# Moving two operand tiles by 128 bytes within a partition of SBUF

## The chip, the cores and the metric

The kernel runs on one core of one Trainium2 chip. The metric is the time of one execution on the device, in microseconds (us).

## The reference

A block of a streaming encoder on 512 tokens of 1024 channels, in float32, with the batch and the depth at 1. Two branches work on the same normed tokens and are merged by gates:

```python
h = rms_norm(x, norm_gain)
proj = einsum('bsd,dc->bsc', h, w_in)            # 1024 -> 10240 columns
sb_q, sb_k, sb_v, sb_g, r_q, r_k, r_v, r_g, m_sb, m_ret = split(proj)

# stick-breaking attention, 8 heads of 128
z = einsum(q, k) * 128 ** -0.5                   # q, k normed per head
log_keep = where(s < t, log_sigmoid(-z), 0)
w = where(s < t, exp(log_sigmoid(z) + sum_later(log_keep)), 0)
out_a = (w @ v) * silu(sb_g)

# retention, 4 heads of 256, rotary q and k, decay gamma_h ** |t - s|,
# causal by chunks of 64
out_b = rms_norm(retention(q, k, v)) * silu(r_g)

p_a, p_b = out_a @ w_branch_sb, out_b @ w_branch_ret
merged = sigmoid(m_sb + b0) * p_a + sigmoid(m_ret + b1) * p_b
out = x + merged @ w_out
```

## The kernel before, in words

Every large product is made in float32r from operands split into two parts, hi and lo: `mm3` (L89) issues three matmuls, hi x hi, hi x lo and lo x hi, into one bank of PSUM. All matmuls go through `matmul` (L84) and all transposes through `transpose` (L87), both kept in the order of the program, so the order of TensorE's work is that of the code.

The transposed tokens are loaded once (`first_loads`, L143), scaled by the gain and split into the two constant tiles xT_hi and xT_lo, each 128 partitions by 8 x 512 values, 16 KB in a partition (L140, L141). They stay for the whole kernel.

`dense` (L209) makes a group of 512 columns: four banks of PSUM, for each of the eight blocks k of 128 channels four times three matmuls, 96 in all, each with 128 x 128 stationary and 128 x 512 moving values. The weights of a group come from `load_split` (L189): pairs of 128 rows are loaded by SyncE's queue into raw, cast to hi by ScalarE and subtracted to lo by VectorE (`split`, L111 to L114), each in two buffers. With rows=True the activations are stationary and the weights moving, otherwise the other way round:

- groups that multiply the tokens (`proj`, L237): qk (4 groups), v and rv (2 each), with the tokens stationary; sg, ma, rg and mb (2 each) and rqk (4), with the tokens moving;
- groups that don't: pa and pb, with the branches' results oa and ob moving; fin, with the merged tokens mg stationary.

Between the pairs of steps of `dense`, `work.step()` takes pieces of side work from a list (`Interleaver`, L38): the transposes of q and k (pqk), the scores of attention (z), the transposes of its weights (pw) and its products with v (po), the scores of retention (rz), its products (ro) and the transposes of its results (rt). Which piece comes where is fixed by counts in the code, not by time. Transposes have a data tile as stationary operand and the constant tile ident as moving one.

Where a tile lies in its partition follows from the order of the `.tile` calls of the constant pool (bufs=1), and behind it the pools wpool (weights), big, tmp and small. Each tile begins at the next multiple of 32 bytes. The order of the constant tiles is wT_0, wT_1 (8192 bytes each), zero, warm (4 bytes each), vec (V_N = 34 values, 136 bytes), xT_hi, xT_lo (16384 each), idle (1024), ident (512), neg_mask (512), m_half (16 values, 64 bytes), rx, rx2 (16 each), rb, cr, sr (2048 each). All tiles of wpool and big are 2048, 4096 or 8192 bytes, so they all begin at the same residue modulo 512.

Of the kernel before, what the change touches and what calls it, by code (L numbers as in the profile page):

```python
# [7 lines left out]
F32 = mybir.dt.float32  # L8
# [4 lines left out]
P = 128  # L13
# [13 lines left out]

V_NG, V_BM, V_QG, V_KG, V_RG, V_N = 0, 8, 24, 25, 26, 34


RAW_BUFS = 2
V_BUFS = 14
# [3 lines left out]


class Interleaver:  # L38
    """Emits a dense stream of products step by step, with pieces of side work between the steps."""

    def __init__(self):
        self.side = []
# [23 lines left out]
def hybrid_block(ctx, tc, x, x_t, vecs, w_in, w_a, w_b, w_o, cos_t, sin_t, decay, out):  # L66
    nc = tc.nc
    PSUM = bass.MemoryType.PSUM

    const = ctx.enter_context(tc.tile_pool(name="const", bufs=1))  # L70
# [7 lines left out]
    work = Interleaver()  # L78
# [8 lines left out]
        tc.keep_in_program_order(nc.tensor.transpose(*a))  # L87

    def mm3(ps, a, b, first, last):  # L89
        """ps += a.T @ b for a and b in two parts each."""  # L90
        matmul(ps, a[0], b[0], start=first, stop=False)
        matmul(ps, a[0], b[1], start=False, stop=False)
        matmul(ps, a[1], b[0], start=False, stop=last)
# [23 lines left out]
        tc.keep_in_program_order(nc.sync.dma_start(dst, src))  # L117

    def load_weights(dst, w, k, n, blocks):
        """n times 128 rows of w, one block of columns or two equal ones."""  # L120
        rows = w[k * P : (k + n) * P, :].rearrange("(a p) c -> p a c", p=P)
        c0, width = blocks[0]
        if len(blocks) == 1:
            load(dst, rows[:, :, c0 : c0 + width])
            return
        step = blocks[1][0] - c0
        for a in range(n):
            src = rows[:, a, c0 - c0 % step : c0 - c0 % step + 2 * step].rearrange("p (b c) -> p b c", b=2)
            load(
                dst[:, a, :].rearrange("p (b c) -> p b c", b=2),  # L130
                src[:, :, c0 % step : c0 % step + width],
            )
# [3 lines left out]
    warm = const.tile([P, 1], F32, name="warm")  # L136
    nc.scalar.activation(warm, zero, AF.Sigmoid)

    vec = const.tile([P, V_N], F32, name="vec")
    xT_hi = const.tile([P, NK, S], F32R, name="xT_hi")  # L140
    xT_lo = const.tile([P, NK, S], F32R, name="xT_lo")  # L141

    def first_loads():  # L143
        """The transposed tokens, and the first weights between them."""
        raws = [wpool.tile([P, 2, S], F32, tag="raw", bufs=RAW_BUFS, name=f"first_raw{k}") for k in range(2)]
        xt = [T_tile(f"xt{hf}", F32) for hf in range(2)]
        for k in range(NK):
            ks = slice(k * P, (k + 1) * P)
            if k < 4:
                load_weights(raws[k // 2][:, k % 2 : k % 2 + 1, :], w_in, k, 1, ((C_Q, 256), (C_K, 256)))  # L150
            load(xt[k // 4][:, k % 4, :], x_t[ks, :])
            if k == 0:
                load(vec, vecs)
        for k in range(NK):
            r = xt[k // 4][:, k % 4, :]
            g = vec[:, V_NG + k : V_NG + k + 1]
            nc.scalar.activation(xT_hi[:, k, :], r, AF.Copy, scale=g)  # L157
            nc.vector.scalar_tensor_tensor(
                xT_lo[:, k, :], r, g, f32(xT_hi[:, k, :]), op0=ALU.mult, op1=ALU.subtract
            )  # L160
        return raws

    first = first_loads()
# [14 lines left out]
    )  # L178
    for t in wT_pair:
        nc.vector.tensor_copy(t[:, NT - 1, (NT - 2) * P : (NT - 1) * P], zero.broadcast_to([P, P]))  # L180
    m_half = const.tile([P, 16], F32, name="m_half")
    nc.gpsimd.memset(m_half, -0.5)

    def rsqrt(dst, ssq, n, width):
# [2 lines left out]
        nc.gpsimd.tensor_tensor(dst, t[:, :width], m_half[:, :width], op=ALU.pow)  # L187

    def load_split(name, w, blocks):  # L189
        """The weights of a group by pairs of 128 rows, in two parts."""  # L190
        for k in range(0, NK, 2):
            with tc.high_priority():
                if name == "qk0" and k < 4:
                    raw = first[k // 2]
                else:
                    raw = wpool.tile([P, 2, S], F32, tag="raw", bufs=RAW_BUFS, name=f"{name}_raw{k}")
                    load_weights(raw, w, k, 2, blocks)
                hi = wpool.tile([P, 2, S], F32R, tag="whi", name=f"{name}_hi{k}")
                lo = wpool.tile([P, 2, S], F32R, tag="wlo", name=f"{name}_lo{k}")
                if name == "qk0" and k < 4:  # L200
                    for j in range(2):
                        nc.vector.tensor_copy(hi[:, j, :], raw[:, j, :])
                        nc.vector.tensor_sub(lo[:, j, :], raw[:, j, :], f32(hi[:, j, :]))
                else:
                    split(hi, lo, raw)
            for j in range(2):
                yield k + j, hi[:, j, :], lo[:, j, :]

    def dense(name, act, w, blocks, rows):  # L209
        """Four PSUM banks: act.T @ w by row blocks, or by column blocks transposed."""  # L210

        ps = [ps_mm.tile([P, S], F32, tag="mm", name=f"{name}_ps{j}") for j in range(4)]
        late = []
        for k, hi, lo in load_split(name, w, blocks):
            if name == "fin1" and k >= NK - 2:
                late.append((k, act(k), (hi, lo)))
                continue
            ahi, alo = act(k)
            if name == "qk0" and k < 2:
                for a, b in ((ahi, hi), (ahi, lo), (alo, hi)):  # L220
                    for j in range(4):
                        matmul(ps[j], a[:, j * P : (j + 1) * P], b, start=k == 0 and a is ahi and b is hi, stop=False)
                continue
            for j in range(4):
                js = slice(j * P, (j + 1) * P)
                if rows:
                    mm3(ps[j], (ahi[:, js], alo[:, js]), (hi, lo), k == 0, k == NK - 1)
                else:
                    mm3(ps[j], (hi[:, js], lo[:, js]), (ahi, alo), k == 0, k == NK - 1)
                if j % 2 == 1 and not (k == NK - 1 and j == 3):  # L230
                    work.step()
        for j in range(4 if late else 0):
            for k, a, b in late:
                mm3(ps[j], [t[:, j * P : (j + 1) * P] for t in a], b, False, k == NK - 1)
        return ps
# [28 lines left out]
        yield 1  # L264

    def token_norm_rows():
        """The tokens' factors along the columns, the same in all partitions."""
        load(cr, cos_t)
        load(sr, sin_t)
        yield 5  # L270
        pr = side_psum("pr")
        for tb in range(NT):
            rc = tmp.tile([P, P], F32, tag="rc", bufs=2, name="rc")
            nc.vector.tensor_copy(rc, rx[:, tb : tb + 1].broadcast_to([P, P]))
            matmul(pr[:, tb * P : (tb + 1) * P], rc, ident, start=True, stop=True)
        nc.vector.tensor_copy(rb, pr)
        nc.gpsimd.tensor_mul(cr, cr, rb)
        nc.gpsimd.tensor_mul(sr, sr, rb)
        yield 1
# [1 line left out]
    qk_parts = {}  # L281

    def qk_group(p):
        """Heads 2p, 2p+1: normed, transposed q and k in two parts: [d, (q0 q1 k0 k1), t]."""
        ps = proj(f"qk{p}", ((C_Q + 256 * p, 256), (C_K + 256 * p, 256)), True)
        ss = small.tile([P, NT, 4], F32, tag="ss", name=f"ss{p}")
        raws = []
# [38 lines left out]
            work.add(token_norm_rows())  # L326

    def v_group(name, c0):
        """Rows of v in two parts, each [s, 512 columns] by row block."""
        ps = proj(name, ((c0, S),), True)  # L330
        got = []
        for sb in range(NT):
            hi = big.tile([P, S], F32R, tag="V", bufs=V_BUFS, name=f"{name}_hi{sb}")
            lo = big.tile([P, S], F32R, tag="V", bufs=V_BUFS, name=f"{name}_lo{sb}")
            r = rx[:, sb : sb + 1]
            nc.scalar.activation(hi, ps[sb], AF.Copy, scale=r)
            nc.vector.scalar_tensor_tensor(lo, ps[sb], r, f32(hi), op0=ALU.mult, op1=ALU.subtract)
            got.append((hi, lo))
        return got
# [25 lines left out]
    oa = {}  # L365

    def attention(heads, ready, v, gates):
        """Stick-breaking attention of some heads, their blocks of 128 queries in a pipeline."""
        blocks = [(h, b) for h in heads for b in range(NT)]
        beta = {}  # L370

# [53 lines left out]
                yield W_W  # L425

    def rope_group(h):
        """Rotated q and k of a head, transposed, in two parts: [d, (q q' k k'), t]."""
        banks = proj(f"rqk{h}", ((C_RQ + 256 * h, 256), (C_RK + 256 * h, 256)), False)
        ps = banks[:2]  # L430
        hi, lo = T_tile(f"rqk_hi{h}"), T_tile(f"rqk_lo{h}")
# [87 lines left out]
    v, sg, rv, rg = {}, {}, {}, {}  # L519
# [17 lines left out]
    for g in range(2):  # L537
        m = gate_group(f"ma{g}", C_MA + S * g, V_BM + 4 * g)
        ps = dense(f"pa{g}", branch_act(oa), w_a, ((S * g, S),), False)
        t = T_tile(f"pa{g}", F32)  # L540
# [26 lines left out]
    for g in range(2):  # L567
        m = mb[g]
        ps = dense(f"pb{g}", branch_act(ob), w_b, ((S * g, S),), False)
        hi, lo = T_tile(f"mg_hi{g}"), T_tile(f"mg_lo{g}")  # L570
        for j in range(4):
            t = tmp_tile(f"mg{g}_{j}")
# [6 lines left out]
    for g in range(2):  # L579
        ps = dense(f"fin{g}", lambda k: tuple(t[:, k % 4, :] for t in mt[k // 4]), w_o, ((S * g, S),), True)  # L580
# [67 lines left out]
```

## Time and profile before

| | |
|---|---|
| median of 3 runs | 671.56 us (670.75 to 671.97) |
| the profiled execution's own time | 671.6 us |
| its span | 671.6 us |
| TensorE busy | 664.3 us, 99% |
| VectorE / ScalarE / GpSimd busy | 375.5 / 260.9 / 50.0 us |
| HBM read | 62.41 MB |

The busy time of TensorE counts a matmul from its start to its modelled end, and matmuls overlap: a matmul of 512 columns is given as some 390 ns, while the next one begins after a little more than half of that. How fast a stretch goes is read from the starts, or from the length of an unbroken stretch divided by the number of its matmuls. A timeline row with "x3" merges three instructions in a row, its time reaching from the first start to the last end.

### The profile page before, as it was taken

Reading aid. Unit: us, or ns where it says so; the run is one execution under the profiler, and the core shown is the slowest. Engines: PE = TensorE matmul, PEld = TensorE weight load, DVE = VectorE, ACT = ScalarE, POOL = GpSimd, SP = SyncE. Lnnn points to the kernel's source line nnn. Section 1 sums busy time; section 2 is a strip of 40 time slices with the busy share of each in tenths; the row PEclk is TensorE's granted clock in tenths of the full one; section 3 lists DMA queues with packets and bytes.
Section 4 is the critical chain, followed back from the end, with each engine's and each line's share of the span. In section 5 each row is a group of like instructions: output and inputs, shape, how many; then the busy total and the mean of one; then the engine's idle time right before and its main releaser. Section 6 shows DMA issues by size and latency. Waiting matters only on the chain.

```text
span 671.6 us, 7979 instructions
## 1 busy us (share of the span) xinstructions
PE 664.3 (99%) x3096; PEld 546.3 (81%) x3096; DVE 375.5 (56%) x560; ACT 260.9 (39%) x416; POOL 50.0 (7%) x50
## 2 busy tenths in 40 slices
PE   8999999999999999999999999999999999999997
PEld 5888888888888888888888888888888888888886
DVE  6346773587487477632333763843863853444632
ACT  4743544464354464421322342433432433422310
POOL 0041000431000300000000001001001001000000
PEclk9999999999999999999999999999999999999999
DMA  8532213222312323132233323222313222234441
GB/s 276 194 125 78 81 62 95 89 69 64 95 62 63 94 63 95 58 99 95 94 95 110 95 63 93 83 91 80 95 63 99 82 86 63 95 94 158 156 157 62
DMA packets 42182, 65.02 MB, mean 97 GB/s; under 512 B 2848, under 2 KB 19488, under 8 KB 42144
## 3 DMA queue, kind: packets, MB, share of 16 engines
q1 hardware_dynamic: 41568, 63.47, 30.3%
q10 hardware_dynamic: 576, 1.05, 0.4%
q8 instruction: 24, 0.39, 0.2%
q14 instruction: 14, 0.11, 0.1%
HBM read 62.41 MB, written 2.10 MB: 96 GB/s over the span
## 4 chain that ended last, share of the span: by engine, by line
PE 98%; DMA 1%; SPq 0%; ACT 0%; DVE 0%; issue 0%; DVEq 0%; ACTq 0%
PE qk_ps L84 14%; PE rqk_ps L84 13%; PE rg_ps L84 7%; PE ma_ps L84 7%; PE mb_ps L84 7%; PE sg_ps L84 7%; PE rv_ps L84 7%; PE v_ps L84 7%; PE pa_ps L84 6%; PE pb_ps L84 6%; PE fin_ps L84 6%; PE po L84 2%; PE rz L84 2%; PE z L84 2%; PE ro L84 2%; PE pw L87 1%
## 5 line engine op out<-in xcount | busy, mean ns | idle before, releaser
L84 PE MATMUL qk_ps<-qk_hi,xT_hi 128*128 128x512 f32 x128 | 51.8, 413 | 2.0 <-ACT xT_hi L157 2.0
L84 PE MATMUL rqk_ps<-xT_hi,rqk_hi 128*128 128x512 f32 x128 | 51.0, 398 | 0.0
L84 PE MATMUL rqk_ps<-xT_hi,rqk_lo 128*128 128x512 f32 x128 | 50.5, 395 | 0.0
L84 PE MATMUL rqk_ps<-xT_lo,rqk_hi 128*128 128x512 f32 x128 | 50.5, 395 | 0.0
L84 PE MATMUL qk_ps<-qk_lo,xT_hi 128*128 128x512 f32 x128 | 50.3, 402 | 0.0
L84 PE MATMUL qk_ps<-qk_hi,xT_lo 128*128 128x512 f32 x128 | 49.6, 395 | 0.0
L84 PE MATMUL pa_ps<-oa,pa_hi 128*128 128x512 f32 x128 | 39.4, 389 | 0.0
L84 PE MATMUL pb_ps<-ob,pb_hi 128*128 128x512 f32 x128 | 39.4, 389 | 0.0
L114 DVE TENSOR_TENSOR rqk_lo<-rqk_raw,rqk_hi 128x1024 fp32r<-128x1024 f32 x16 | 20.6, 1288 | 24.4 <-ACT rqk_hi L113 24.4
L384 DVE TENSOR_TENSOR_SCAN keep<-keep,zero 128x128 f32<-128x128 f32 (+3 forms) x32 | 27.1, 846 | 7.3 <-ACT keep L382 7.3
L84 PEld LDWEIGHTS qk_ps<-qk_hi,xT_hi 128*128 128x128 f32 x128 | 24.5, 192 | 7.7 <-ACT xT_hi L157 2.9
L84 PEld LDWEIGHTS qk_ps<-qk_hi,xT_lo 128*128 128x128 f32 x128 | 24.3, 190 | 5.7
L84 PEld LDWEIGHTS rqk_ps<-xT_hi,rqk_lo 128*128 128x128 f32 x128 | 24.1, 188 | 5.7
L84 PEld LDWEIGHTS qk_ps<-qk_lo,xT_hi 128*128 128x128 f32 x128 | 24.7, 193 | 4.7
L84 PEld LDWEIGHTS rqk_ps<-xT_lo,rqk_hi 128*128 128x128 f32 x128 | 24.1, 188 | 5.2
L84 PEld LDWEIGHTS rqk_ps<-xT_hi,rqk_hi 128*128 128x128 f32 x128 | 24.1, 188 | 5.2
L84 PEld LDWEIGHTS pa_ps<-oa,pa_hi 128*128 128x128 f32 x128 | 24.0, 188 | 5.1
L84 PEld LDWEIGHTS pb_ps<-ob,pb_hi 128*128 128x128 f32 x128 | 24.0, 188 | 5.0
L187 POOL TENSOR_TENSOR rrr<-ms,m_half 128x4 f32<-128x4 f32 x4 | 4.0, 1006 | 321.5 <-DVE ms L186 321.5
L113 ACT CAST rqk_hi<-rqk_raw 128x1024 fp32r<-128x1024 f32 x16 | 16.8, 1047 | 26.4 <-PE rqk_ps L84 17.0
L114 DVE TENSOR_TENSOR qk_lo<-qk_raw,qk_hi 128x1024 fp32r<-128x1024 f32 x14 | 17.3, 1235 | 16.3 <-ACT qk_hi L113 16.3
L84 PE MATMUL v_ps<-v_hi,xT_hi 128*128 128x512 f32 x64 | 26.3, 411 | 0.0
(185 smaller groups left out, 1711.9 us busy)
## 6 DMA issues: line engine op xcount, KB each, us to landing
rqk_raw<-in_w_in SPq DMA_DIRECT2D x32, 256.0 KB, 3.0
qk_raw<-in_w_in SPq DMA_DIRECT2D x28, 256.0 KB, 3.1
v_raw<-in_w_in SPq DMA_DIRECT2D x8, 512.0 KB, 3.7
sg_raw<-in_w_in SPq DMA_DIRECT2D x8, 512.0 KB, 3.7
rv_raw<-in_w_in SPq DMA_DIRECT2D x8, 512.0 KB, 3.7
ma_raw<-in_w_in SPq DMA_DIRECT2D x8, 512.0 KB, 3.7
pa_raw<-in_w_a SPq DMA_DIRECT2D x8, 512.0 KB, 3.7
rg_raw<-in_w_in SPq DMA_DIRECT2D x8, 512.0 KB, 3.7
```

The source lines that it names most:

```text
L84: tc.keep_in_program_order(nc.tensor.matmul(*a, **k))
L87: tc.keep_in_program_order(nc.tensor.transpose(*a))
L113: nc.scalar.copy(hi, src)
L114: nc.vector.tensor_sub(lo, src, f32(hi))
L187: nc.gpsimd.tensor_tensor(dst, t[:, :width], m_half[:, :width], op=ALU.pow)
L384: nc.vector.tensor_tensor_scan(keep[:, :n][:, ::-1], keep[:, :n][:, ::-1], zero.broadcast_to([P, n]), 1.0, op0=ALU.mult, op1=ALU.add,)
```

## The change

The constant tiles vec and m_half are allocated wider, and their first columns are used as before. vec takes 66 values (264 bytes) in place of 34, m_half 112 values (448 bytes) in place of 16. With steps of 32 bytes xT_hi, xT_lo, idle, ident, neg_mask and m_half begin 128 bytes later, and all tiles behind m_half 512 bytes later. Some comments (docstrings) are taken out as well, each leaving an empty line.

```diff
 V_NG, V_BM, V_QG, V_KG, V_RG, V_N = 0, 8, 24, 25, 26, 34
 
+V_ROOM, M_ROOM = 66, 112
+
...
-    vec = const.tile([P, V_N], F32, name="vec")
+    vec = const.tile([P, V_ROOM], F32, name="vec")[:, :V_N]
     xT_hi = const.tile([P, NK, S], F32R, name="xT_hi")
     xT_lo = const.tile([P, NK, S], F32R, name="xT_lo")
...
-    m_half = const.tile([P, 16], F32, name="m_half")
+    m_half = const.tile([P, M_ROOM], F32, name="m_half")[:, :16]
     nc.gpsimd.memset(m_half, -0.5)
```

## Rows read from the trace of the kernel before

**Rows 1.** The page: span, busy time by engine, the chain's shares.
```profile
span 671.6 us, 7979 instructions
...
PE 664.3 (99%) x3096; PEld 546.3 (81%) x3096; DVE 375.5 (56%) x560; ACT 260.9 (39%) x416; POOL 50.0 (7%) x50
...
PE 98%; DMA 1%; SPq 0%; ACT 0%; DVE 0%; issue 0%; DVEq 0%; ACTq 0%
```

**Rows 2.** TensorE's waits: total us, times, longest.
```profile
PE qk_ps L84 <- ACT xT_hi L157: 2.0, 1, 2.0
PE pi L84 <- DVE idle L166: 1.2, 1, 1.2
```

**Rows 3.** The chain's longest pieces: start us, us, what, matmuls.
```profile
98.48 25.10 PE qk_ps L84 x108
167.40 12.60 PE sg_ps L84 x54
...
301.98 22.39 PE ma_ps L84 x96
324.37 21.77 PE pa_ps L84 x96
346.14 22.39 PE rqk_ps L84 x96
...
624.08 43.53 PE fin_ps L84 x192
```

**Rows 4.** Windows: busy PE, PEld, DVE, ACT, POOL, clock, DMA share, GB/s.
```profile
301.80:324.20 22.40, 22.40 (x97) 18.02 (x96) 7.68 (x9) 5.35 (x6) 0.00 (x0) 1.00 0.30 95
324.20:346.00 21.80, 21.80 (x98) 18.04 (x97) 7.65 (x9) 5.64 (x8) 0.00 (x0) 1.00 0.31 96
```

**Rows 5.** Groups by line and form: xcount, busy us, mean ns.
```profile
L84 PE MATMUL qk_ps<-qk_hi,xT_hi 128*128 128x512 f32 x128 | 51.8, 413 | 2.0 <-ACT xT_hi L157 2.0
...
L87 PE MATMUL pw<-ident,beta 128*128 128x128 f32 x80 | 13.9, 272 | 0.0
...
L84 PEld LDWEIGHTS rqk_ps<-xT_hi,rqk_hi 128*128 128x128 f32 x128 | 24.1, 188 | 5.2
L84 PEld LDWEIGHTS pa_ps<-oa,pa_hi 128*128 128x128 f32 x128 | 24.0, 188 | 5.1
...
L87 PEld LDWEIGHTS pw<-ident,beta 128*128 128x128 f32 x80 | 10.5, 140 | 3.6
```

**Rows 6.** Timeline of PE, the start: start us, us, instruction.
```profile
6.79 2.08 PE L84 MATMUL qk_ps<-qk_hi,xT_hi 128*128 128x512 f32 x4 [2.01 <-ACT xT_hi L157]
...
10.37 1.21 PE L84 MATMUL qk_ps<-qk_hi,xT_lo 128*128 128x512 f32 x4
```

**Rows 7.** Timeline of PE: first and fifth triple of pa0, each from its start.
```profile
280.01 0.62 PE L84 MATMUL pa_ps<-oa,pa_hi 128*128 128x512 f32 x2
...
282.77 0.62 PE L84 MATMUL pa_ps<-oa,pa_hi 128*128 128x512 f32 x2
```

**Rows 8.** Timeline of PE: six score matmuls of retention, then rg.
```profile
380.97 0.39 PE L84 MATMUL rz<-rqk_hi 128*128 128x512 f32 x1
...
381.67 0.39 PE L84 MATMUL rz<-rqk_hi 128*128 128x512 f32 x1
...
382.35 0.40 PE L84 MATMUL rg_ps<-xT_hi,rg_hi 128*128 128x512 f32 x1
```

**Rows 9.** Timeline of PE: first and last cut into xT groups.
```profile
43.48 0.60 PE L87 MATMUL pqk<-ident,qraw 128*128 128x128 f32 x4
...
575.75 0.60 PE L87 MATMUL rt<-ident,roraw 128*128 128x128 f32 x4
```

**Rows 10.** Timelines of ACT and DVE: one pair of weights in ma1.
```profile
307.37 1.05 ACT L113 CAST ma_hi<-ma_raw 128x1024 fp32r<-128x1024 f32 x1 [4.54 <-PE ma_ps L84]
...
308.46 1.23 DVE L114 TENSOR_TENSOR ma_lo<-ma_raw,ma_hi 128x1024 fp32r<-128x1024 f32 x1 [4.37 <-ACT ma_hi L113]
```

**Rows 11.** Timeline of DVE at the start: third pair of qk0.
```profile
16.16 1.22 DVE L114 TENSOR_TENSOR qk_lo<-qk_raw,qk_hi 128x1024 fp32r<-128x1024 f32 x1 [0.88 <-ACT qk_hi L113]
```

## The prediction

> **What bounds the kernel now.** I read the page first: TensorE is busy for 664.3 of 671.6 us, and it makes up 98% of the chain that ended last [rows 1]. Then its waits: in the whole span it waited 3.2 us for others, all of it at the start [rows 2]. So nothing feeds it late, and the time is the sum of the distances from one matmul's start to the next. A busy share of 99% does not say that this distance is the shortest possible; that has to be read from stretches in which nothing but 512-column matmuls runs.
>
> The chain's longest pieces are such stretches, and here the reader should divide time by count [rows 3]. In groups that read the transposed tokens (xT_hi, xT_lo): ma and rqk 22.39 / 96 = 233.2 ns, sg 12.60 / 54 = 233.3, qk 25.10 / 108 = 232.4. In the groups that don't read them: pa 21.77 / 96 = 226.8, fin 43.53 / 192 = 226.7. The shapes are the same, two-part float32r, 128x128 against 128x512, three products per tile. Nor is it the load on other engines: the window in ma1 has DVE 7.68 us, ACT 5.35 and DMA 0.30 busy, that in pa1 right behind it DVE 7.65, ACT 5.64 and DMA 0.31 [rows 4]; yet the distance goes 233.2 (ma), 226.8 (pa), 233.2 (rqk) in direct succession. Nor is it the role of the tokens: they are stationary in qk and v, moving in ma, sg, rg and rqk, and both kinds are slow; the weights are moving in fin and stationary in pa, and both are fast.
>
> What is left is where the operands lie. By the sizes in the code, with each tile on a multiple of 32 bytes, what stands between xT and the weights' tiles is 1024 + 512 + 512 + 64 + 32 + 32 + 3 x 2048 bytes, which is 128 modulo 512; every later tile of two KiB or more keeps the weights' residue. So pa, pb and fin multiply operands of one residue, and every xT group operands 128 bytes apart. While one matmul streams its moving operand, the next one's weight load (188 ns in every group) reads its stationary one [rows 5]; I take the distance to depend on how those two reads lie to each other. The 226.8 and the 233.2 ns are the evidence; the mechanism behind is inferred.
>
> **The change, part by part.**
>
> The room behind vec (136 to 264 bytes, that is 160 to 288 with the 32-byte steps) moves xT_hi and xT_lo by 128, and idle, ident, neg_mask and m_half with them. The room behind m_half (64 to 448 bytes) adds 384, so that all later tiles move by 512 and keep their residue. No instruction, DMA, wait or order changes: the same columns of vec are loaded, the same 16 columns of m_half are set. These edits cost nothing in themselves, and need no cover.
>
> *Gain.* Matmuls with xT number 3 x 128 in qk [rows 5], by the code as many in rqk, and 3 x 64 for each of v, sg, rv, ma, rg and mb: 384 + 384 + 6 x 192 = 1920. The first eight take from 6.79 to 10.37 us, 0.45 us each [rows 6], another level than the two above; I leave out these and the one behind them: 1911. From 232.4 to 233.3, taken as 232.8 because both values fill about as many stretches, to 226.7 is 6.1 ns each: 1911 x 6.1 = 11.7 us. Bounds: 5.7 ns (from 232.4) is 10.9 us, 6.6 ns is 12.6 us.
>
> *What takes some of it back.* A fast group does not start fast. pa0's first twelve matmuls take 2.76 us, from 280.01 to 282.77, against 12 x 0.2267 = 2.72, so 0.04 lost [rows 7]. The scores of retention, whose operands all have one residue too, settle sooner: 0.70 us for the first three and 0.68 for the next three, 0.02 lost [rows 8]. Side work (transposes, scores) cuts the xT groups into many stretches: read through, the timeline has 124, the first cut at 43.48 and the last at 575.75 us [rows 9]; 85 of them are six matmuls long, 21 are 12 or 18, and 18 longer. At 0.02 us per stretch that is 2.5 us. At the other end the stretches of six never settle: they lose 510 x 6.1 = 3.1 us, and the other 39 lose 0.04 each, as pa0, 1.6 us, together 4.7. At the near end it is nothing. I take 2.5, since the retention stretch is the row that resembles a six-matmul stretch most.
>
> *The transposes.* Their moving operand ident comes to the residue of their stationary ones. They number 80 for pw [rows 5] and by the code 64 for pqk and 32 for rt, 176 in all, each 128 columns wide. No row shows such a pair, so I bound it by the effect per 512-column matmul, 6.1 ns either way: 1.1 us more or less, taken as nothing, since nothing decides the sign and the weight load is another one there, 140 ns in place of 188 [rows 5].
>
> *Covers.* The cast and the subtraction of a pair of weight rows follow the release of a buffer and end 2.3 us later (307.37 to 308.46 + 1.23), while TensorE has another pair's 24 matmuls in hand, 5.6 us [rows 10]. At 226.7 ns these are 5.44 us, so some 3 us remain. At the start the third pair of qk weights is ready at 16.16 + 1.22 = 17.38 us [rows 11]; TensorE comes to it after 48 matmuls from 6.79 us, near 19.6, and would come 0.25 us earlier. Neither cover goes. The end (fin, then the last output) is unchanged and shifts whole.
>
> **Sum**, against the profiled execution: its time is its span of 671.6 us, with nothing around it, and the median of the runs shown is 671.56, so that the sum holds for both. 671.6 - 11.7 + 2.5 = 662.4 us. Its own range is 659.0 (12.6 gained, nothing given back) to 664.6 (11.7 - 4.7), and the transposes may add 1.1 at either end.
>
> **Rivals.**
>
> *Residue means nothing, 671.6 us.* The slow groups would be slow for something else in xT, its place below 51 KB or its being one 16 KB tile. Against it: the scores of attention and retention read one large tile against itself or its other half, and do reach 0.68 us per three [rows 8]; the low address is not excluded by any row. The trace shows 226.8 against 233.2 ns on equal load, which already is a dependence on the operands [rows 3, 4]. [...]
>
> *Only one role gains.* If the moving operand's own place counts, the groups with xT moving (384 + 4 x 192 = 1152) gain 7.0 us less 1.5 at the starts of stretches (their share of the 2.5): 666.1 us. If only the stationary one's counts, 768 matmuls gain 4.7 less 1.0: 667.9. Against both: in qk as in ma the slow distance appears although one of the two operands is where fin and pa have it.
>
> *Slower, 683.3 us.* The equal residue makes the two reads of TensorE meet in the same place and each matmul loses once more what separates the two levels, 6.1 ns: 1911 x 6.1 = 11.7 us on top, in every xT group. It decides if the distance in ma1 rises above 233 ns, at once visible as over 22.4 us per 96. The distances of pa and fin, at equal residue, speak against it [rows 3].
>
> **How the numbers follow.** Forecast 0.81, one role only 0.07, no effect 0.07, slower 0.05. The time is the forecast's, 662.4. The range goes from the forecast's lower bound to the nearer one-role case, which takes in the transposes at the upper end: 659.0 to 666.2. A measurement of this kernel can tell some 0.2% (1.3 us) from no change. Faster 0.88, same 0.07, slower 0.05.
>
> **What the profile after would show.** Right: ma1's 96 matmuls in 21.8 us, qk's 108 in 24.5, sg's 54 in 12.3; pa, pb and fin as before; 188 ns weight loads; waits of TensorE still about 3 us. The stretches of six tell the start cost: 1.36 us plus 0.02 is right, 1.40 means that they never settle. Wrong: ma1 still at 22.39 (no effect), qk changed and ma not or the reverse (one role), or new waits of TensorE on the cast or the subtraction of weights.

## The result, and the profile after

The change makes the kernel faster: 663.64 us in the median of 4 runs (662.98 to 664.30) against 671.76 us (4 runs, 670.75 to 672.78), a ratio of 0.9878 with a 95% interval of 0.9861 to 0.9896. Run again later beside the kernel before, on one chip, it had 664.14 against 670.96 us, 0.9893 (0.9877 to 0.9909).

The page of the kernel after: span, busy time by engine, the chain's shares.

```profile
span 662.4 us, 7979 instructions
...
PE 656.3 (99%) x3096; PEld 546.4 (82%) x3096; DVE 375.9 (57%) x560; ACT 260.7 (39%) x416; POOL 50.8 (8%) x50
...
PE 99%; DMA 0%; SPq 0%; ACT 0%; DVE 0%; issue 0%; DVEq 0%; ACTq 0%
```

TensorE is still at 99% and still makes the whole chain, as in [rows 1]. Neither its share nor its count of instructions tells that anything has changed; only its busy time and the span do. TensorE's waits after, in total us, times and longest:

```profile
PE pi L86 <- DVE idle L168: 1.2, 1, 1.2
PE qk_ps L86 <- ACT xT_hi L159: 0.9, 1, 0.9
```

The wait for the first tokens is 1.1 us shorter than in [rows 2]. That belongs to the execution, not to the change: the wait is for a load (ScalarE begins xT_hi after 2.65 us of waiting for vec, at 4.87 us), and in the runs below it lies between 0.5 and 1.8 us. The longest pieces of the chain, with start, time and number of matmuls, answer to [rows 3]:

```profile
96.32 24.50 PE qk_ps L86 x108
164.41 12.24 PE sg_ps L86 x54
...
297.84 21.76 PE ma_ps L86 x96
319.60 21.76 PE pa_ps L86 x96
341.36 21.76 PE rqk_ps L86 x96
...
614.93 43.53 PE fin_ps L86 x192
```

Here is the change: ma and rqk went from 22.39 to 21.76 us, exactly pa's time, sg from 12.60 to 12.24, qk from 25.10 to 24.50. All of them now divide to 226.7 to 226.9 ns per matmul. pa and fin, whose operands moved together, are where they were. The windows of ma1 and pa1 (busy time of PE, PEld, DVE, ACT, POOL, then clock, DMA share, GB/s) answer to [rows 4]:

```profile
297.70:319.40 21.70, 21.70 (x97) 18.01 (x96) 7.58 (x9) 5.24 (x6) 0.00 (x0) 1.00 0.34 97
319.40:341.10 21.70, 21.70 (x97) 17.98 (x96) 7.58 (x9) 5.66 (x7) 0.00 (x0) 1.00 0.32 98
```

The other engines do as much as before, in a shorter time. The weight load itself, in the groups by line and form, is not faster than in [rows 5], so the 6 ns did not come out of it:

```profile
L86 PEld LDWEIGHTS rqk_ps<-xT_hi,rqk_hi 128*128 128x128 f32 x128 | 24.1, 188 | 4.7
```

What the change did not give shows in the timeline of TensorE, in three stretches of rg1, each behind scores of retention (start us, us, instruction; a stretch reaches from its first row to the row of what follows it):

```profile
480.70 0.39 PE L86 MATMUL rg_ps<-xT_hi,rg_hi 128*128 128x512 f32 x1
...
483.42 0.33 PE L86 MATMUL rz<-rqk_hi 128*128 128x384 f32 x1
...
484.49 0.39 PE L86 MATMUL rg_ps<-xT_hi,rg_hi 128*128 128x512 f32 x1
...
487.25 0.28 PE L86 MATMUL rz<-rqk_hi 128*128 128x256 f32 x1
...
491.42 0.40 PE L86 MATMUL rg_ps<-xT_hi,rg_hi 128*128 128x512 f32 x1
...
492.81 0.39 PE L86 MATMUL rqk_ps<-xT_hi,rqk_hi 128*128 128x512 f32 x1
```

The first stretch follows six 512-column products and takes 2.72 us for twelve matmuls, 226.7 ns each. The second, behind products of 384 columns, takes 2.76 us, and the third, behind products of 256, takes 1.39 us for six, 231.7 ns each: in these three a cut costs something where the width changes at it, 0.04 and 0.03 us over 226.7 ns per matmul, and nothing where it stays at 512 columns.

### The profile page after: what moved, and what is told of

Same layout as the page of the kernel before. It is cut to its first block, busy times and chain, and to the rows that moved or that the text cites. A ratio compares the mean times of both kernels' runs of the same rounds, so it can differ in the third digit from the quotient of the medians.

```text
span 662.4 us, 7979 instructions
## 1 busy us (share of the span) xinstructions
PE 656.3 (99%) x3096; PEld 546.4 (82%) x3096; DVE 375.9 (57%) x560; ACT 260.7 (39%) x416; POOL 50.8 (8%) x50
## 4 chain that ended last, share of the span: by engine, by line
PE 99%; DMA 0%; SPq 0%; ACT 0%; DVE 0%; issue 0%; DVEq 0%; ACTq 0%
PE qk_ps L86 14%; PE rqk_ps L86 13%; PE sg_ps L86 7%; PE v_ps L86 7%; PE ma_ps L86 7%; PE rv_ps L86 7%; PE mb_ps L86 7%; PE rg_ps L86 7%; PE fin_ps L86 7%; PE pb_ps L86 7%; PE pa_ps L86 7%; PE po L86 2%; PE z L86 2%; PE rz L86 2%; PE ro L86 2%; PE pw L89 1%
```

## The experiments

Eight of the kernels below differ from the changed one in the two numbers of rooms alone:

```diff
-V_ROOM, M_ROOM = 66, 112
+V_ROOM, M_ROOM = 66, 16      # first room only
+V_ROOM, M_ROOM = 34, 112     # second room only
+V_ROOM, M_ROOM = 130, 48     # tokens 256 bytes before the weights
+V_ROOM, M_ROOM = 98, 80      # tokens 128 behind
+V_ROOM, M_ROOM = 82, 96      # tokens 64 behind
+V_ROOM, M_ROOM = 50, 128     # tokens 64 before
+V_ROOM, M_ROOM = 74, 104     # tokens 32 behind
+V_ROOM, M_ROOM = 90, 88      # tokens 96 behind
```

The theory was that the distance between a matmul's moving operand and the stationary one of the next, modulo some power of two, sets the pace. The rivals were the tokens' own place, and one operand's place alone. All stationary tiles of a group have one residue, so no run here can tell a matmul's own stationary operand from that of the next: what the runs compare is the residue of the moving tiles with that of the stationary ones.

**First room only.** 

> Only the room behind vec: the tokens stay at their new place (residue 480 modulo 512), but the weights and all other late tiles move 128 bytes on as well (residue 96), so that the two are 128 apart again. If the distance between the two operands modulo 512 decides: as the kernel before, 671 to 672 us, 96 matmuls of ma1 in 22.4 us, and pa and fin still at 226.7 ns. If the tokens' own place decides: as the changed kernel, 663 to 664 us, ma1 in 21.8 us.

Measured: 671.42 us in the median against 671.23 for the kernel before, ratio 0.9999 (0.9981 to 1.0017). Its chain's pieces:

```profile
97.51 25.10 PE qk_ps L86 x108
...
300.95 22.39 PE ma_ps L86 x96
323.34 21.77 PE pa_ps L86 x96
```

The tokens lie where the changed kernel has them, and nothing is gained: their own place is not it.

**Second room only.** 

> Only the room behind m_half: the tokens stay where the kernel before has them (residue 352), and the weights and all other late tiles come to 352 too. If the distance between the operands decides: as the changed kernel, 663 to 664.5 us, ma1's 96 matmuls in 21.8 us. If the tokens' own old place is the slow one: ma1 in 22.4 us and 671 to 672 us. If residue 480 itself is the fast one: pa and fin slow as well, above 232 ns each.

Measured: 663.60 us, ratio 0.9881 (0.9857 to 0.9905). Its chain's pieces:

```profile
95.20 24.52 PE qk_ps L86 x108
...
296.88 21.76 PE ma_ps L86 x96
318.64 21.76 PE pa_ps L86 x96
```

The tokens lie at their old address, below 51 KB in one 16 KB tile, and the whole gain is there, because the weights came to them. The two halves, each run alone, decide the matter: the first leaves the operands 128 bytes apart, the second brings them together.

**256 bytes apart.** 

> The tokens 256 bytes before the weights modulo 512 (residues 224 and 480). If only equality modulo 512 is fast: over 232 ns per matmul in ma1, 671 us or more. If the distance counts modulo 256 alone: 226.7 ns, 663 to 664 us.

Measured: 663.17 us, ratio 0.9868 (0.9852 to 0.9884). Its chain's pieces:

```profile
94.91 24.50 PE qk_ps L86 x108
...
296.40 21.76 PE ma_ps L86 x96
318.16 21.76 PE pa_ps L86 x96
```

So the residue modulo 256 is enough; the change asked for more than it needed.

**128 bytes the other way.** 

> The tokens 128 bytes behind the weights (residues 96 and 480) in place of 128 before them. If only equality is fast, or if the sign does not count: over 232 ns per matmul in ma1, 671 us or so. If it is enough that the moving operand is not behind the stationary one, one of the two kinds of groups (qk with the tokens stationary, ma with the tokens moving) is fast and the other slow, 666 to 668 us.

Measured: 671.06 us, ratio 0.9999 (0.9985 to 1.0013). Its chain's pieces:

```profile
96.17 25.10 PE qk_ps L86 x108
...
299.66 22.39 PE ma_ps L86 x96
322.05 21.77 PE pa_ps L86 x96
```

It is the kernel before again, to the hundredth of a microsecond per piece, as a period of 256 asks: 128 behind is 128 before.

**64 bytes, both ways.** Behind: 

> The tokens 64 bytes behind the weights modulo 512. If blocks of 128 bytes with a period of 256 decide and both reads run through whole periods, 64 bytes may lie anywhere between the two levels: 226.7 ns if half a block apart is as good as none, 232 to 233 if any distance costs the whole step, some 230 if it goes by the distance. Time 663 to 672 us accordingly; 667 by the middle.

Before: 

> The tokens 64 bytes before the weights modulo 512. The same three cases as with 64 bytes behind; if the sign counts, the two differ by more than 1 us, with the tokens' stationary groups (qk, v, rv) on one side and the moving ones (sg, ma, rqk, rg, mb) on the other.

Measured, one run each: 670.42 us with the tokens behind and 671.12 with the tokens before; the kernel before had 672.48 in the median of 7 beside them. The chain's pieces with the tokens 64 behind:

```profile
97.83 25.20 PE qk_ps L86 x108
...
301.60 21.99 PE ma_ps L86 x96
```

and with the tokens 64 before:

```profile
97.02 24.74 PE qk_ps L86 x108
...
299.62 22.40 PE ma_ps L86 x96
```

Divided by the counts: tokens behind, qk 233.3 and ma 229.1 ns; tokens before, qk 229.1 and ma 233.3. The two are mirror images, as qk has the tokens stationary and ma has them moving: with the moving operand 64 bytes behind the stationary one it is 229.1 ns in either, with the moving one 64 before 233.3. The two times differ by only 0.7 us, less than the 1 us that was asked of them: the kernel has 768 and 1152 matmuls of the two kinds, so that most of the two effects cancels in the time. The pieces show it clearly all the same.

**32 and 96 bytes behind.** 

> The tokens 32 bytes behind the weights modulo 512. With 64 behind, the groups with the tokens moving (ma, rqk) were at 229.1 ns and those with the tokens stationary (qk) at 233.3; with 64 before, the other way round. If the cost grows with the distance of the moving operand behind the stationary one: ma between 226.7 and 229.1 (21.76 to 21.99 us per 96), and qk at 233 or between 227 and 233. If any distance but none loses: both over 229 ns. If zero is not the best place: ma or qk below 226.7.

> The tokens 96 bytes behind the weights modulo 512. If the cost goes by distance modulo 256: ma between 229.1 (at 64) and 233.2 ns (at 128), that is 21.99 to 22.39 us per 96, and qk, 96 the other way, between 232.4 and 233.3. If the steps are of 64 bytes: ma at 229.1 as with 64, or at 233 as with 128.

Measured, one run each: 672.23 and 672.95 us, slower than the kernel before, which had 670.96 in the median of 7 beside them. The chain's pieces with 32 bytes:

```profile
96.47 25.19 PE qk_ps L86 x108
...
300.19 22.40 PE ma_ps L86 x96
```

and with 96:

```profile
96.71 25.30 PE qk_ps L86 x108
...
300.85 22.41 PE ma_ps L86 x96
```

The cost does not grow with the distance: 32 bytes already cost all. Each ma and qk piece gives one value of the moving operand's residue minus the stationary one's, modulo 256:

| moving minus stationary | ns per matmul | read from |
|---|---|---|
| 0 | 226.7 to 227.0 | changed kernel, 256 before, second room only |
| 32 | 233.3 | 32 behind, ma |
| 64 | 229.1 | 64 behind, ma; 64 before, qk |
| 96 | 233.4 | 96 behind, ma |
| 128 | 232.4 to 233.2 | kernel before and 128 behind, qk and ma |
| 160 | 234.3 | 96 behind, qk |
| 192 | 233.3 | 64 before, ma; 64 behind, qk |
| 224 | 233.2 | 32 behind, qk |

Equality is the best of the eight; no step of 32 bytes beats it. The rows other than 0 and 128 rest on one profiled run each, or two.

**Half the cuts.** In `dense`, two steps of side work after twelve matmuls in place of one after six:

```diff
-                if j % 2 == 1 and not (k == NK - 1 and j == 3):
+                if j == 3 and k < NK - 1:
+                    work.step()
+                    work.step()
+                elif j == 1 and k == NK - 1:
                     work.step()
```

> As the changed kernel, but side work is let in after twelve matmuls, two pieces at a time, in place of one piece after six; the pieces and their order stay. If each cut costs some 27 ns at the start of the next stretch (85 stretches of six carry 2.24 us over 226.7 ns per matmul), about 1 us goes: 662.6 us. If what is lost goes by matmuls under side work and not by cuts: no change, 663.6. If a second piece has to wait for the first one's bank or buffer: TensorE waits appear, and it is slower than 664 us.

Measured: 666.65 us, ratio 0.9905 (0.9888 to 0.9922). The changed kernel's ratio is 0.9878 (0.9861 to 0.9896), so this one is some 2 us slower by its ratio, on another chip, with intervals that just overlap. The profiled executions say the same: from the first product of the tokens to the end it is 658.9 us here and 656.8 in the changed kernel. It has a wait that none of the others has:

```profile
PE pw L89 <- DVE beta L393: 1.6, 4, 0.5
```

Two pieces in a row do wait for the chain behind the first, as the third case had it. The first case was not wrong about the starts: read from the starts in the timeline (as explained under Gain below), the stretches behind the very first lose 2.58 us over 226.7 ns per matmul with half the cuts against 3.37 with all, 0.8 us less, near the 1 us it asked for. The waits took back more than that. The 53 stretches of 12 to 18 matmuls lose 1.84 us here, 35 ns each, against 26 ns for each of the 85 stretches of six in the changed kernel: the joined stretch loses more than one of six, so that joining two saves 17 of 52 ns, less than half of what they lose.

**ident back.** 

> As the changed kernel, but ident and neg_mask are back at residue 352, where the kernel before has them. If the transposes' distance does not depend on it: four transposes still take 0.35 us, and the time is that of the changed kernel, 663 to 664.3. If the stretches behind transposes start as they do because ident lies on the tokens' residue: their excess of 2.24 us changes by more than 0.3 us, either way.

```diff
-V_ROOM, M_ROOM = 66, 112
+V_ROOM, M_ROOM = 66, 16
...
-    idle = const.tile([P, S], mybir.dt.bfloat16, name="idle")
+    idle = const.tile([P, S + 192], mybir.dt.bfloat16, name="idle")[:, :S]
```

Measured, one run: 665.01 us, beside 672.48 for the kernel before. TensorE waited for xT_hi twice in its start, 1.7 us in all. The stretches of six lose 2.67 us in place of 2.24, and in second room only, where ident lies with everything else, 2.46. The 0.43 us are more than the 0.3 that the second case asked for, but half of them also appear between two kernels that both have ident at equal residue. One run leaves it open whether ident's place costs anything; it shows no more than 0.4 us.

**wT too.** 

> As the changed kernel, but the two constant tiles wT, which take part in the products po and ro, are moved to the residue of the other tiles as well (128 to 480 modulo 512), by placing zero before them with some room. If equality modulo 256 is what counts in every product: po's 24 matmuls of 512 columns and the stretches behind them gain up to 6 ns each, the 256-column products of ro 1 to 2 ns, together 0.2 to 0.5 us: 663.2 us. If small products are bound by something else: no change from the changed kernel.

```diff
-V_ROOM, M_ROOM = 66, 112
+V_ROOM, M_ROOM = 120, 112
...
+    zero = const.tile([P, 88], F32, name="zero")[:, :1]
     wT_pair = [const.tile([P, NT, S], F32R, name=f"wT_{q}") for q in range(2)]
...
-    zero = const.tile([P, 1], F32, name="zero")
```

**The changed kernel again**, beside it. 

> The changed kernel once more, beside the one before it, so that the two are compared on one chip: 663.6 us, 8 us below the kernel before.

Measured: 664.36 us with wT moved and 664.14 without, ratios to the kernel before of 0.9900 (0.9883 to 0.9916) and 0.9893 (0.9877 to 0.9909). There is nothing to be had in the small products: the 24 matmuls of po with 512 columns take 5.95 us in place of 5.99, and the other products are within 0.1 us. No version here beats the changed kernel; the 663.17 of 256 bytes apart is the same within its interval.

## Why the prediction was right

**The bound, and what sets the distance.** Read from the chain's pieces, the 226.7 and the 233 ns were two levels of one operation, and the change brought every long piece from one to the other. That the distance between the operands does it, and not the place of either, is now shown by the two halves of the change run alone; before, it was inferred. The rivals fall one by one: the low address and the large tile by second room only, one role alone by 64 bytes both ways and by qk and ma both gaining, the slower case by every piece at equal residue. The weight load is 188 ns in most groups, but not in every one, as the prediction says: on the page of the kernel before it is 190 to 193 in qk's. Nothing hangs on that. Kernels that differ in addresses alone take from 226.7 to 234.3 ns per matmul. The trace shows that a weight load runs under the matmul ahead of its own: in ma1 of the kernel before, the load for the matmul that begins at 302.51 us begins at 302.28 and takes 0.19 us, under a matmul of 0.40 us from 302.27. That it is these two reads that disturb each other is the prediction's inference; no view shows it, and the mechanism stays open.

**Gain.** 11.7 us were forecast for 1911 matmuls at 6.1 ns. Read from the starts, the matmuls behind the first ten stood 16.1 us above 226.7 ns each before, and stand 7.9 above it after, 8.2 less. Part of both is the transposes': the last transpose of a piece is followed by the next start after 25 to 30 ns, 28 in the median, the others after 109, and the matmul behind it has 0.31 to 0.32 us to the next start, before and after alike. In the kernel before, behind the first four transposes [rows 9]:

```profile
43.84 0.48 PE L84 MATMUL v_ps<-v_hi,xT_hi 128*128 128x512 f32 x1
44.16 0.39 PE L84 MATMUL v_ps<-v_lo,xT_hi 128*128 128x512 f32 x1
```

All sums over stretches in this text leave out 80 ns at each place behind a transpose, 57 in these two kernels. So counted, 11.6 us stood above 226.7 ns before and 3.4 do after. In the long pieces ma, rqk and sg gained 6.5 to 6.6 ns per matmul and qk 5.6, on either side of the 6.1.

**What takes some of it back.** This term was the one mis-sized: 2.5 us forecast, 3.4 measured. That it came so near is partly luck, since the rows it was taken from show something else. In [rows 8] the first three scores of retention took 0.70 us. In the changed kernel they take 0.68, like the next three, which end at the 480.70 shown above:

```profile
479.34 0.39 PE L86 MATMUL rz<-rqk_hi 128*128 128x512 f32 x1
...
480.02 0.39 PE L86 MATMUL rz<-rqk_hi 128*128 128x512 f32 x1
```

pa0's first twelve matmuls [rows 7] take 2.72 us after, in place of 2.76. Both losses came from the group ahead, whose operands lay 128 bytes apart, and went with the change; "a fast group does not start fast" was a wrong reading of them. What is lost now goes by the width of what stands ahead: 57 stretches behind transposes lose 1.80 us (32 ns each), 40 behind products of 256 columns 1.03 (26 ns), 12 behind 384 columns 0.48 (40 ns), and 14 behind 512 columns only 0.06 (4 ns); the very first stretch loses nothing behind its first ten matmuls. Over all 124 stretches it is 27 ns in place of 20: 2.24 us in 85 stretches of six, 0.63 in 21 of 12 or 18, 0.51 in 18 longer ones. The stretches of six gained only 1.8 ns per matmul, from 232.9 to 231.1. The bound at that end (stretches of six gain nothing, 4.7 us) held.

**The transposes, the covers.** Nothing there moved: pw's 80 transposes have 272 ns as in [rows 5], four of them still take 0.35 us, and TensorE waits for no cast or subtraction.

**Sum.** 662.4 us forecast, 663.64 measured. The spans say 9.2 us gained (671.6 to 662.4) and the medians 8.1. The difference lies at the start: the first product of the tokens begins at 6.79 us in [rows 6] and at 5.65 us after,

```profile
5.65 2.08 PE L86 MATMUL qk_ps<-qk_hi,xT_hi 128*128 128x512 f32 x4 [0.87 <-ACT xT_hi L159]
```

and from there to the end it is 664.8 and 656.8 us, 8.0 less, which is 11.6 - 3.4 = 8.2 within 0.2. The forecast's 9.2 gained was thus 1.1 us too much, of which the starts of stretches are 0.9. One step of it was wrong in itself, though it cost nothing: an execution's time is not its span. After, the profiled execution has 664.18 us for a span of 662.4, 1.8 us more, and in every run for which both are on record it is 1.7 to 1.9 us, so the profiled execution of the kernel before was probably slower than the median of its runs by about that.

## What to carry to other kernels

A TensorE that was 99% busy lost 3% of each long piece here (22.39 us for 96 matmuls in place of 21.76), 1.2% of the whole kernel, to where its operands lie: divide the chain's long pieces by their counts, compare groups of one shape, and where they differ with equal load on the other engines, work out the residues of the moving and the stationary tiles modulo 256 bytes (equal, 226.7 ns per matmul here; 32 to 224 bytes apart, 229.1 to 234.3). A small constant tile ahead of a large one is enough to set them apart, and some room behind it to bring them together. Then count the cuts: matmuls that are interrupted every six gained 1.8 ns here, less than a third of the 5.6 to 6.6 that long stretches gained.

## What was not expected of the hardware

- In the steps of 32 bytes tried here, all in float32r, the pace follows the difference of the two residues with a period of 256 bytes, not 512 (226.7 ns at 256 bytes apart as at 0, in ma 233.2 at 128 either way), and is neither gradual nor symmetric: 32 bytes cost as much as 128 (233.3 ns), while the moving operand 64 bytes behind the stationary one costs 2.4 ns (229.1) and 64 before costs 6.6 (233.3).
- In the changed kernel, stretches of twelve matmuls and more start slowly behind products or transposes of another width. Behind 256 columns the first five distances from start to start are 229.1 to 235.1 ns in the mean and the next six 226.4 to 226.9; behind 384 columns the first nine are 228.5 to 234.9 and the next two 226.4 and 226.5. The stretches of 12 to 18 lose 32 ns on the way behind 256 columns and 43 behind 384; behind products of 512 columns they lose 0.5 ns. Behind transposes, stretches of any length lose 32 ns.
- With no cut between them, ma1, pa1 and rqk0 now run through at one pace: in the changed kernel pa begins at 226.7 ns.
